# A one-core decoder block: layer norm by running sums less a pivot, and the shift sums of two GLU row blocks moved from TensorE to VectorE

## Chip, cores and metric

One Trainium2 chip, one core. The metric is device time in microseconds (us) of one execution; lower is better. Engines are TensorE (PE), VectorE (DVE), ScalarE (ACT), GpSimd (POOL) and SyncE (SP, which here only issues loads). All inputs are float32 in HBM, the input and output activations are 256 x 2048.

## What is computed

One layer of a hybrid decoder block and a final RMSNorm. Cut to what matters here:

```python
ada = (silu(c) @ w_ada + b_ada)            # (1, 6*2048)
sh1, sc1, g1, sh2, sc2, g2 = split(ada, 6)
h = rmsnorm(x, norm1_g) * (1 + sc1) + sh1
proj = h @ w_in                            # queries, keys, values, gates, GLU input, merge gates
y_a = attention(...) @ w_o_nsa
a, g = split(glu_in, 2)
u = a * sigmoid(g)                         # 256 x 2048
u = causal_dwconv(u, width 31) + bias
u = silu(layernorm over the 2048 channels (u) * ln_g + ln_b)
y_b = u @ conv_pw_w + b_pw
x = x + g1 * ((sigmoid(ga) * y_a + sigmoid(gb) * y_b) @ w_out)
h = rmsnorm(x, norm2_g) * (1 + sc2) + sh2
x = x + g2 * conv_ffn(h);  return rmsnorm(x, final_g)
```

## The kernel before

**Weights.** Every weight matrix is streamed once, in tiles of 128 x 1024 values (512 KB) that SP loads into `raw` (four buffers). ACT makes `hi`, the value rounded to the matmul's format (L227), DVE makes `lo`, the remainder (L228), three buffers each, and TensorE multiplies three times: activation-hi by hi, activation-hi by lo, activation-lo by hi (L249 to L251, L261 to L264; L282 and L283 pair two of them). There are 546 such tiles. Counted in the order of use: 64 for the GLU (1 to 64), 122 for keys, values, queries, the first merge gate and the attention's output product (65 to 186), 32 for the second merge gate `gbs` (187 to 218), 32 for `conv_pw_w` (219 to 250), 32 for `w_out` (251 to 282), then the FFN. Because there are three hi and three lo buffers, the tiles 219 to 221 can be split before TensorE is through with tile 218, and tile 221 only when tile 218 has been used.

**The GLU in four quarters.** The GLU's 64 tiles are taken in four row blocks (quarters) of 512 rows of `w_in`, because the rows of `h` become known a quarter at a time: `ada_quarter(q)` sums the shift and scale of quarter q from `w_ada` while the product of quarter q-1 runs. The scale side (side 1) is summed on DVE (`ada_dve`, L439, one fused multiply-add of 128 x 512 per 128 rows), the shift side (side 0) on TensorE (`ada_pe`, L421, matmuls with 32 weight columns, in four column groups). `modulate` then turns both into columns and makes the next rows of `h` (L375 to L378, L350, L351). `glu_out` adds each partial product in PSUM to `u` or `gl` (L390).

**Work in between.** The depthwise convolution, the layer norm and the other sums over `w_ada` are fillers: lists of small steps (`conv_q`, `ada_q`) with a declared cost. After each tile `tick` hands out steps as long as their engines' declared load is not ahead of TensorE's. An `ada_q` step loads one 128 x 1024 tile of `w_ada` into `araw` (two buffers, on the same SP queue as `raw`) and adds it on DVE (L298 first, then L301). Once `norm_only` is set, `ada_q` waits until `conv_q` is empty. A scheduler in the compiler then writes each engine's instruction order from its own time model; `high_priority` moves steps forward in it.

**Convolution.** `conv_blocks` takes three of the 16 channel blocks at a time (then the last alone): ACT multiplies by a tap (L559) and DVE adds (L568), or DVE does both (L549); the last tap writes the result back into `u` (L566). Two `cacc` buffers let two groups overlap.

**Layer norm.** After the last convolution group, DVE sums all 16 blocks (L880 to L886, then `half_sum`, L875 and L876), one matmul with ones gives the mean over channels, L898 subtracts it in place from all of `u`, ACT squares (L901), DVE sums, a second matmul (L909) gives the variance, eight 256-wide steps (L911 to L917) make the inverse deviation, L923 scales, ACT applies scale, bias and SiLU (L929), and L350 and L351 split the result into `uT`, the activation of the `conv_pw_w` product. `conv_done`, which is put before the layer norm, closes the convolution's pool, sets `norm_only`, and adds the 32 steps of the gate `g1` to the front of `ada_q`; their sums end in a matmul with ones (L326) and in `gb` (L327), which `residual` (L1010) needs in the `w_out` product. What is left of `conv_q` is emitted (`drain`) between tiles 218 and 219; what is left of the 32 gate steps, before `w_out`.

Of the kernel before, what the change touches and what calls it, by code (L numbers as in the profile page):

```python
# [59 lines left out]
def block_kernel(ctx, tc, x, c, w_ada, b_ada, norm1_g, w_in, cmp_pe, w_kc1, w_kc2, w_vc1, w_vc2,  # L60
# [82 lines left out]
    def give(q):  # L143
        cost, f = q.popleft()
        use(**cost)
        with ExitStack() as es:
            es.enter_context(tc.issue_after(los[0]))
            if q is heads_q:
                es.enter_context(tc.high_priority(HP))
            f()  # L150
# [250 lines left out]
    with tc.tile_pool(name="first", bufs=4) as first:  # L401
# [41 lines left out]
        def ada_quarter(q):  # L443
            box = {}
            js = range(q * KQ // 2, (q + 1) * KQ // 2)
            turns = [ada_dve(box, q, 1), (x for j in js for x in ada_pe(box, j, 0))]
            for _ in range(8):
                for g in turns:
                    next(g)
                    yield  # L450
            for g in turns:
                for _ in g:
                    pass
            for n, j in enumerate(js):
                modulate(j, halves(box[0, j]) + halves(box[1][:, n * T:(n + 1) * T]))
                yield
# [74 lines left out]
    MANY, FEW = tuple(s for s in range(2, CW) if s % 6) + (1,), tuple(range(6, CW, 4)) + (1,)  # L531

    def conv_blocks(b0, n, WIDE):

# [3 lines left out]
        def first(b):  # L538
            def f():
                if b == b0:  # L540
                    box["a"] = cvp.tile([P, n, T], F32, tag="cacc", name=nm("cacc"), bufs=2)
                nc.scalar.activation(box["a"][:, b - b0, :], u[:, b, :], AF.Identity, bias=cvb[:, b:b + 1],
                                     scale=cw[:, CW - 1, b:b + 1])
# [314 lines left out]
    def conv_done():  # L858

        cv.__exit__(None, None, None)  # L860
        norm_only[0] = True
        late = ctx.enter_context(tc.tile_pool(name="late", bufs=1))
# [4 lines left out]

    conv_q.append(({}, conv_done))


    lb = {}

    def half_sum(dst, a):

        nc.vector.tensor_add(a[:, 0:2, :], a[:, 0:2, :], a[:, 2:4, :])  # L875
        nc.vector.tensor_add(dst, a[:, 0, :], a[:, 1, :])  # L876

    def ln_mean1():
        lb["a"] = t4([P, 4, T])
        nc.vector.tensor_add(lb["a"], u[:, 0:4, :], u[:, 4:8, :])  # L880

    def ln_mean2():
        nc.vector.tensor_add(lb["a"], lb["a"], u[:, 8:12, :])

    def ln_mean3():
        nc.vector.tensor_add(lb["a"], lb["a"], u[:, 12:16, :])  # L886

    def ln_mean4():
        half_sum(lb["a"][:, 0, :], lb["a"])
        mp = pt([P, T])  # L890
        nc.tensor.matmul(mp, ones, lb["a"][:, 0, :], start=True, stop=True)
        lb["m"] = mp
        lb["q"] = t4([P, 4, T])

    def ln_centre(j):
        def f():
            v = u[:, 4 * j:4 * j + 4, :]
            nc.vector.scalar_tensor_tensor(v, lb["m"][:, None, :].to_broadcast([P, 4, T]), -1.0 / D, v,  # L898
                                           op0=ALU.mult, op1=ALU.add)
            s4 = t4([P, 4, T])  # L900
            nc.scalar.activation(s4, v, AF.Square)  # L901
            half_sum(lb["q"][:, j, :], s4)
        return f

    def ln_var():
        q = lb["q"]
        half_sum(q[:, 0, :], q)
        vp = pt([P, T])
        nc.tensor.matmul(vp, ones, q[:, 0, :], start=True, stop=True)  # L909
        ve = t4([P, 4, T])  # L910
        nc.vector.tensor_scalar(ve[:, 0, :], vp, 1.0 / D, EPS, op0=ALU.mult, op1=ALU.add)  # L911
        nc.scalar.activation(ve[:, 1, :], ve[:, 0, :], AF.Sqrt)
        nc.vector.reciprocal(ve[:, 2, :], ve[:, 1, :])
        nc.vector.tensor_mul(ve[:, 3, :], ve[:, 2, :], ve[:, 2, :])
        nc.vector.tensor_mul(ve[:, 3, :], ve[:, 3, :], ve[:, 0, :])
        nc.vector.tensor_scalar(ve[:, 3, :], ve[:, 3, :], -0.5, 1.5, op0=ALU.mult, op1=ALU.add)
        nc.vector.tensor_mul(ve[:, 3, :], ve[:, 3, :], ve[:, 2, :])  # L917
        lb["r"] = ve[:, 3, :]

    def ln_scale(j):  # L920
        def f():
            v = u[:, 4 * j:4 * j + 4, :]
            nc.vector.tensor_tensor(v, v, lb["r"][:, None, :].to_broadcast([P, 4, T]), op=ALU.mult)  # L923
        return f
# [7 lines left out]
    def ln_split(j):  # L932
        def f():
            if j == 0:
# [3 lines left out]
        return f  # L938

    conv_q.extend(({"dve": d, "act": a}, f) for d, a, f in  # L940
                  [(1130, 0, ln_mean1), (1130, 0, ln_mean2), (1130, 0, ln_mean3), (900, 0, ln_mean4)]
                  + [(2000, 1050, ln_centre(j)) for j in range(4)] + [(3000, 1700, ln_var)]
                  + [(1130, 0, ln_scale(0))]
                  + [i for j in range(4) for i in [(1130, 0, ln_scale(j + 1))] * (j < 3)
                     + [(0, LN_SILU, ln_silu(4 * j)), (0, LN_SILU, ln_silu(4 * j + 2))]])

# [194 lines left out]
```

## Time and profile before

| | |
|---|---|
| median of 3 runs | 1765.69 us (1760.31 to 1766.15) |
| the profiled execution | 1763.86 us, its span 1762.1 us |
| TensorE busy | 1696.0 us, 96% |
| VectorE busy | 1315.4 us, 75% |
| ScalarE busy | 992.1 us, 56% |
| loads | 403.85 MB read, 230 GB/s over the span |
| largest wait of TensorE | 16.3 us, one time, at 784.6 us |

The page gives busy time by engine and the chain of work that ended last. The waits name what an engine sat idle for. The timeline lists instructions in order of time with the idle time before each in square brackets. A table of stretches gives busy time, granted TensorE clock and DMA rate of each stretch.

### The profile page before, as it was taken

How to read it: one execution, taken by the hardware profiler on the slowest of the kernel's cores; microseconds unless marked ns; L12 is line 12 of the kernel's file. 1: busy time of each engine (PE TensorE's matmuls, PEld its weight loads, DVE VectorE, ACT ScalarE, POOL GpSimd, SP SyncE). 2: the span in 40 equal slices, each digit the busy share in tenths (PEclk: the TensorE clock that was granted, in tenths of full speed). 3: DMA queues.
4: the chain of work that ended last, by engine and by line, in shares of the span. 5: the costliest groups of instructions: out<-in, count | busy, mean ns of one | idle time of the engine just before them, and what ended most of it. 6: DMA issues, size and time to landing. Idle time of an engine off the chain costs nothing.

```text
span 1762.1 us, 26526 instructions
## 1 busy us (share of the span) xinstructions
PE 1696.0 (96%) x10148; PEld 1468.2 (83%) x10148; DVE 1315.4 (75%) x1722; ACT 992.1 (56%) x1506; POOL 6.2 (0%) x28
## 2 busy tenths in 40 slices
PE   6999999999999999987999899999999999999997
PEld 4899999999887778865877888888988888898886
DVE  2677698898878899988897677776577776576665
ACT  4443576885677778755344565554455554345553
POOL 0000000000000000000000000000000000000000
PEclk8999999999999999998999999999999999999998
DMA  9999788877557346778898577776677765566653
GB/s 342 321 352 321 233 276 273 269 249 215 178 163 245 131 150 209 238 227 279 312 315 298 180 229 225 221 223 221 223 225 222 220 215 180 191 191 189 189 191 124
DMA packets 264362, 407.68 MB, mean 231 GB/s; under 512 B 12684, under 2 KB 156844, under 8 KB 263596
## 3 DMA queue, kind: packets, MB, share of 16 engines
q1 hardware_dynamic: 261676, 399.44, 69.9%
q10 hardware_dynamic: 2560, 6.55, 1.1%
q8 instruction: 79, 1.29, 0.3%
q14 instruction: 47, 0.39, 0.1%
HBM read 403.85 MB, written 2.10 MB: 230 GB/s over the span
## 4 chain that ended last, share of the span: by engine, by line
PE 87%; DMA 5%; DVE 4%; ACT 2%; issue 2%; SPq 0%; ACTq 0%; DVEq 0%
PE accp L282 18%; PE accx L250 12%; PE accx L249 11%; PE accx L251 11%; PE accp L283 9%; PE accw L261 6%; PE accw L264 6%; PE accw L263 6%; DMA araw<-in_w_ada_dram 3%; DVE t L301 1%; PE pt L788 1%; DVE lo L228 1%; PE pt L421 1%; PE pt L827 1%; DMA araw<-in_w_kc_dram 1%
## 5 line engine op out<-in xcount | busy, mean ns | idle before, releaser
L227 ACT CAST hi<-raw 128x1024 fp32r<-128x1024 f32 x546 | 572.1, 1048 | 639.7 <-PE accx L251 266.7
L228 DVE TENSOR_TENSOR lo<-raw,hi 128x1024 fp32r<-128x1024 f32 x546 | 665.5, 1220 | 317.8 <-ACT hi L227 314.3
L282 PE MATMUL accp<-act,hi 128*128 128x512 f32 x1408 | 495.5, 397 | 0.2
L249 PE MATMUL accx<-hi,act 128*128 128x512 f32 (+2 forms) x1176 | 429.1, 366 | 18.3 <-ACT act L350 17.7
L250 PE MATMUL accx<-lo,act 128*128 128x512 f32 (+2 forms) x1176 | 435.0, 370 | 3.9 <-DVE lo L228 3.7
L251 PE MATMUL accx<-hi,act 128*128 128x512 f32 (+2 forms) x1176 | 429.3, 365 | 0.8 <-DVE act L351 0.8
L283 PE MATMUL accp<-act,lo 128*128 128x256 f32 x1408 | 395.2, 281 | 0.2 <-DVE lo L228 0.2
L282 PEld LDWEIGHTS accp<-act,hi 128*128 128x128 f32 x1408 | 264.2, 188 | 64.1 <-DVE act L351 0.8
L249 PEld LDWEIGHTS accx<-hi,act 128*128 128x128 f32 x1176 | 222.8, 189 | 55.1 <-ACT act L350 18.6
L283 PEld LDWEIGHTS accp<-act,lo 128*128 128x128 f32 x1408 | 266.0, 189 | 0.8 <-DVE lo L228 0.6
L261 PE MATMUL accw<-act,hi 128*128 128x256 f32 x896 | 259.1, 290 | 4.9 <-ACT accw L587 2.8
L250 PEld LDWEIGHTS accx<-lo,act 128*128 128x128 f32 x1176 | 222.9, 190 | 45.3 <-DVE lo L228 9.7
L263 PE MATMUL accw<-act,hi 128*128 128x256 f32 x896 | 258.0, 288 | 0.0
L264 PE MATMUL accw<-act,lo 128*128 128x256 f32 x896 | 257.6, 288 | 0.2 <-DVE lo L228 0.2
L251 PEld LDWEIGHTS accx<-hi,act 128*128 128x128 f32 x1176 | 223.0, 190 | 36.7 <-issue 1.7
L261 PEld LDWEIGHTS accw<-act,hi 128*128 128x128 f32 x896 | 174.8, 195 | 11.7 <-issue 3.9
L264 PEld LDWEIGHTS accw<-act,lo 128*128 128x128 f32 x896 | 174.5, 195 | 3.9 <-issue 3.1
L263 PEld LDWEIGHTS accw<-act,hi 128*128 128x128 f32 x896 | 174.6, 195 | 3.5 <-issue 3.0
L301 DVE SCALAR_TENSOR_TENSOR t<-araw,cs,t 128x1024 f32<-128x1024 f32 x120 | 153.5, 1279 | 19.2 <-DMA araw<-in_w_ada_dram 18.9
L559 ACT ACTIVATE cprod<-big,cw 128x230 f32<-128x230 f32 (+27 forms) x298 | 124.6, 487 | 13.4 <-DVE cacc L568 11.3
L568 DVE TENSOR_TENSOR cacc<-cacc,cprod 128x726 f32<-128x726 f32 (+28 forms) x110 | 87.6, 797 | 11.4 <-ACT cprod L559 8.2
L549 DVE SCALAR_TENSOR_TENSOR cacc<-big,cw,cacc 128x232 f32<-128x232 f32 (+24 forms) x182 | 77.6, 463 | 0.6
(208 smaller groups left out, 1051.2 us busy)
## 6 DMA issues: line engine op xcount, KB each, us to landing
araw<-in_w_ada_dram SPq DMA_DIRECT2D x192, 512.0 KB, 5.0
raw<-in_w_in_dram SPq DMA_DIRECT2D x180, 512.0 KB, 4.9
raw<-in_ffn_w_up_dram SPq DMA_DIRECT2D x176, 512.0 KB, 4.5
raw<-in_ffn_w_down_dram SPq DMA_DIRECT2D x88, 512.0 KB, 3.7
raw<-in_w_o_nsa_dram SPq DMA_DIRECT2D x32, 512.0 KB, 3.7
raw<-in_conv_pw_w_dram SPq DMA_DIRECT2D x32, 512.0 KB, 5.6
raw<-in_w_out_dram SPq DMA_DIRECT2D x32, 512.0 KB, 5.2
araw<-in_w_kc_dram SPq DMA_DIRECT2D x8, 512.0 KB, 5.6
```

The costliest lines, as they stand in the source:

```text
L227: nc.scalar.copy(hi[:, :n], raw[:, :n])
L228: los.append(nc.vector.tensor_tensor(lo[:, :n], raw[:, :n], hi[:, :n], op=ALU.subtract).ins)
L249: nc.tensor.matmul(o, act[:, k, 0, s], hi, start=k == 0, stop=False)
L250: nc.tensor.matmul(o, act[:, k, 0, s], lo, start=False, stop=False)
L251: nc.tensor.matmul(o, act[:, k, 1, s], hi, start=False, stop=k == nk - 1)
L261: nc.tensor.matmul(acc[:, b, :], hi[:, s], act[:, k, 0, :], start=begin and k == first and b % 2 == 0, stop=False, skip_group_check=True)
L263: nc.tensor.matmul(acc[:, b, :], hi[:, s], act[:, k, 1, :], start=False, stop=False, skip_group_check=True)
L264: nc.tensor.matmul(acc[:, b, :], lo[:, s], act[:, k, 0, :], start=False, stop=last, skip_group_check=True)
L282: nc.tensor.matmul(acc[:, b], hi[:, s], act[:, k], start=k == 0, stop=False, skip_group_check=True)
L283: nc.tensor.matmul(acc[:, b, 0, :], lo[:, s], act[:, k, 0, :], start=False, stop=k == KB - 1, skip_group_check=True)
L301: nc.vector.scalar_tensor_tensor(acc, raw, cs[:, k:k + 1], acc, op0=ALU.mult, op1=ALU.add)
L559: nc.scalar.mul(box["p"][:, b - b0, s:], u[:, b, :T - s], cw[:, CW - 1 - s, b:b + 1])
```

## The change

Three things are changed, all in the code above. (1) The shift sums of quarters 2 and 3 are made by `ada_dve` as well, so TensorE sums only quarter 1's. (2) The layer norm is computed by running sums: after the first convolution group a pivot (the mean of its three blocks) is found; each group, once convolved, has the pivot subtracted and is added, with its square, to two running sums `sq` while the convolution goes on; at the end one matmul gives both sums, the variance is mean of squares less squared mean, and `ln_scale` subtracts the mean and scales. (3) `cacc` has one buffer, `conv_done` and `norm_only` come after `ln_var`, and convolution-queue steps get high priority from then on.

```diff
-            if q is heads_q:
+            if q is heads_q or q is conv_q and norm_only[0]:
                 es.enter_context(tc.high_priority(HP))
...
+            on_pe = q < 2
+            turns = [ada_dve(box, q, 1), (x for j in js for x in ada_pe(box, j, 0)) if on_pe else ada_dve(box, q, 0)]
...
+                shift = box[0, j] if on_pe else box[0][:, n * T:(n + 1) * T]
+                modulate(j, halves(shift) + halves(box[1][:, n * T:(n + 1) * T]))
...
+    sq = cvp.tile([P, 2, T], F32, name="sq")
+    pivot = cvp.tile([P, T], F32, name="pivot")
+    def norm_sums(b0, n):
+        def sums(dst, a, fresh):
+            if fresh:
+                nc.vector.tensor_add(dst, a[:, 0, :], a[:, 1, :])
+            for j in range(2 if fresh else 0, n):
+                nc.vector.tensor_add(dst, dst, a[:, j, :])
+        def find():
+            sums(sq[:, 0, :], u[:, :n, :], True)
+            p_ = pt([P, T])
+            nc.tensor.matmul(p_, ones, sq[:, 0, :], start=True, stop=True)
+            nc.scalar.mul(pivot, p_, 1.0 / (n * P))
+        def less():
+            v = u[:, b0:b0 + n, :]
+            nc.vector.tensor_tensor(v, v, pivot[:, None, :].to_broadcast([P, n, T]), op=ALU.subtract)
+        def add():
+            v = u[:, b0:b0 + n, :]
+            s4 = t4([P, n, T])
+            nc.scalar.activation(s4, v, AF.Square)
+            sums(sq[:, 0, :], v, b0 == 0)
+            sums(sq[:, 1, :], s4, b0 == 0)
+        if b0 == 0:
+            conv_q.append(({"dve": 900, "act": 450, "pe": 250}, find))
+        conv_q.append(({"dve": 170 + n * 265}, less))
+        conv_q.append(({"dve": 840 * n, "act": 250 + 200 * n}, add))
...
-                    box["a"] = cvp.tile([P, n, T], F32, tag="cacc", name=nm("cacc"), bufs=2)
+                    box["a"] = cvp.tile([P, n, T], F32, tag="cacc", name=nm("cacc"))
...
+        norm_sums(b0, n)
...
     def conv_done():
-        norm_only[0] = True
...
     def ln_var():
+        norm_only[0] = True
+        vp = pt([P, 2, T])
+        nc.tensor.matmul(vp.rearrange("p a t -> p (a t)"), ones, sq.rearrange("p a t -> p (a t)"), start=True, stop=True)
         ve = t4([P, 4, T])
+        nc.vector.tensor_scalar(ve[:, 3, :], vp[:, 0, :], 1.0 / D, None, op0=ALU.mult)
+        nc.vector.tensor_mul(ve[:, 2, :], ve[:, 3, :], ve[:, 3, :])
+        nc.vector.scalar_tensor_tensor(ve[:, 0, :], vp[:, 1, :], 1.0 / D, ve[:, 2, :], op0=ALU.mult, op1=ALU.subtract)
+        nc.vector.tensor_scalar(ve[:, 0, :], ve[:, 0, :], EPS, None, op0=ALU.add)
...
     def ln_scale(j):
             v = u[:, 4 * j:4 * j + 4, :]
+            nc.vector.tensor_tensor(v, v, lb["m"][:, None, :].to_broadcast([P, 4, T]), op=ALU.subtract)
             nc.vector.tensor_tensor(v, v, lb["r"][:, None, :].to_broadcast([P, 4, T]), op=ALU.mult)
...
+    conv_q.append(({"dve": 5500, "act": 500}, ln_var))
+    conv_q.append(({}, conv_done))
```

The layer norm's old steps (`ln_mean1` to `ln_mean4`, `ln_centre`, `half_sum`) are gone.

The scheduler rewrites the order of every engine. Three places:

VectorE in the second GLU quarter (`asum` is a running sum over `w_ada`, `araw` its loaded tile, `accw` a GLU partial product). Before, from the fourth L390 of that quarter back:

```order
L439 SCALAR_TENSOR_TENSOR asum_1058<-araw_1302,cs,asum_1058 128x512
L228 TENSOR_TENSOR lo_1236<-raw_1234,hi_1235 128x1024
L439 SCALAR_TENSOR_TENSOR asum_1058<-araw_1302,cs,asum_1058 128x512
L439 SCALAR_TENSOR_TENSOR asum_1058<-araw_1374,cs,asum_1058 128x512
L228 TENSOR_TENSOR lo_1266<-raw_1264,hi_1265 128x1024
L439 SCALAR_TENSOR_TENSOR asum_1058<-araw_1374,cs,asum_1058 128x512
L390 TENSOR_TENSOR big_269<-big_269,accw_1155 128x1024
```

Now:

```order
L439 SCALAR_TENSOR_TENSOR asum_1058<-araw_1359,cs,asum_1058 128x512
L228 TENSOR_TENSOR lo_1226<-raw_1224,hi_1225 128x1024
L439 SCALAR_TENSOR_TENSOR asum_1063<-araw_1293,cs,asum_1063 128x512
L439 SCALAR_TENSOR_TENSOR asum_1058<-araw_1359,cs,asum_1058 128x512
L228 TENSOR_TENSOR lo_1256<-raw_1254,hi_1255 128x1024
L439 SCALAR_TENSOR_TENSOR asum_1063<-araw_1293,cs,asum_1063 128x512
L390 TENSOR_TENSOR big_269<-big_269,accw_1149 128x1024
L439 SCALAR_TENSOR_TENSOR asum_1058<-araw_1367,cs,asum_1058 128x512
L439 SCALAR_TENSOR_TENSOR asum_1063<-araw_1363,cs,asum_1063 128x512
```

Two running sums alternate where one stood; over the quarter twice as many L439 stand between the L228 of its 16 tiles.

VectorE at the end of the merge-gate product (the only L228 in each piece is tile 221's; `big_268` is `u`, `pt` the sums in PSUM, `t_1259` and `t_1275` the deviation's steps). Before, where the last convolution result (L566) had stood at tile 208:

```order
L911 TENSOR_SCALAR t_1259_7920<-pt_7918 128x256
L298 TENSOR_SCALAR t_1296_8159<-araw_8157,cs 128x1024
L913 RECIPROCAL t_1259_7920<-t_1259_7920 128x256
L301 SCALAR_TENSOR_TENSOR t_1296_8159<-araw_8161,cs,t_1296_8159 128x1024
L228 TENSOR_TENSOR lo_8237<-raw_8235,hi_8236 128x1024
L914 TENSOR_TENSOR t_1259_7920<-t_1259_7920 128x256
L301 SCALAR_TENSOR_TENSOR t_1296_8159<-araw_8182,cs,t_1296_8159 128x1024
L915 TENSOR_TENSOR t_1259_7920<-t_1259_7920 128x256
L301 SCALAR_TENSOR_TENSOR t_1296_8159<-araw_8208,cs,t_1296_8159 128x1024
L916 TENSOR_SCALAR t_1259_7920<-t_1259_7920 128x256
L917 TENSOR_TENSOR t_1259_7920<-t_1259_7920 128x256
L923 TENSOR_TENSOR big_268<-big_268,t_1259_7920 128x1024 x4
```

Now:

```order
L228 TENSOR_TENSOR lo_8216<-raw_8214,hi_8215 128x1024
L605 TENSOR_TENSOR cacc_7697<-cacc_7697,cprod_7955 128x229
L605 TENSOR_TENSOR cacc_7697<-cacc_7697,cprod_7958 128x228
L605 TENSOR_TENSOR cacc_7697<-cacc_7697,cprod_7961 128x227
L603 TENSOR_TENSOR big_268<-cacc_7697,cprod_7964 128x256
L556 TENSOR_TENSOR big_268<-big_268,pivot 128x256
L546 TENSOR_TENSOR sq<-sq,big_268 128x256
L546 TENSOR_TENSOR sq<-sq,t_1273_8010 128x256
L914 TENSOR_SCALAR t_1275_8016<-pt_8014 128x256
L929 TENSOR_TENSOR big_268<-big_268,t_1275_8016 128x1024 x2
L915 TENSOR_TENSOR t_1275_8016<-t_1275_8016 128x256
```

Behind the last row stand, now, two more L929, L916, L917, the reciprocal L919, L920 to L923, four L930 and four L351, and then tile 222. So the last convolution result (L603), the sums, the variance and the scaling all stand behind tile 221's L228, where L911 and L913 stood ahead of it; no gate step (L298, L301) stands among them, and the first of those now stands at tile 230 where it stood at tile 220.

SP's queue of loads in the `w_out` product (`raw` is a weight tile, `araw` a step over `w_ada`). Before, around its eighteenth `raw`:

```order
L224 DMA raw_9257<-in_w_out_dram 128x2x512
L295 DMA araw_9116<-in_w_ada_dram 128x1024
L224 DMA raw_9275<-in_w_out_dram 128x2x512
L295 DMA araw_9137<-in_w_ada_dram 128x1024
L224 DMA raw_9293<-in_w_out_dram 128x2x512
```

Now:

```order
L224 DMA raw_9264<-in_w_out_dram 128x2x512
L295 DMA araw_8935<-in_w_ada_dram 128x1024
L295 DMA araw_9011<-in_w_ada_dram 128x1024
L295 DMA araw_9039<-in_w_ada_dram 128x1024
L224 DMA raw_9282<-in_w_out_dram 128x2x512
L295 DMA araw_9060<-in_w_ada_dram 128x1024
L295 DMA araw_9081<-in_w_ada_dram 128x1024
L295 DMA araw_9084<-in_w_ada_dram 128x1024
L224 DMA raw_9309<-in_w_out_dram 128x2x512
```

From the eighteenth gate step to the last step over `w_ada` ahead of the second norm, 24 `araw` loads now stand with 19 `raw` loads, where 17 stood with the same 19; and the second L326, which waits for the 32nd gate step, stands on TensorE in tile 262, ahead of tiles 257 and 258, where it stood in tile 253.

## Rows read from the trace of the kernel before

**Rows 1.** The page, part 1: the span, then busy us (share) xinstructions of each engine

```profile
span 1762.1 us, 26526 instructions
...
PE 1696.0 (96%) x10148; PEld 1468.2 (83%) x10148; DVE 1315.4 (75%) x1722; ACT 992.1 (56%) x1506; POOL 6.2 (0%) x28
```

**Rows 2.** The page, part 4: shares of the chain that ended last, by engine

```profile
PE 87%; DMA 5%; DVE 4%; ACT 2%; issue 2%; SPq 0%; ACTq 0%; DVEq 0%
```

**Rows 3.** Waits on PE: waiter <- waited for: us in total, times, longest

```profile
PE accx L249 <- ACT act L350: 17.7, 2, 16.3
```

**Rows 4.** Stretches: PE, PEld, DVE, ACT, POOL busy; granted clock, DMA share, GB/s

```profile
92.85:201.99 109.14, 108.90 (x935) 100.50 (x934) 77.82 (x94) 43.40 (x53) 0.91 (x1) 1.00 0.91 302
202.00:784.60 582.60, 575.54 (x3532) 503.76 (x3530) 502.91 (x738) 421.51 (x785) 2.67 (x12) 0.99 0.69 219
784.60:800.90 16.30, 0.03 (x1) 0.04 (x1) 14.34 (x16) 10.87 (x16) 0.00 (x0) 0.66 0.64 211
800.90:838.00 37.10, 34.41 (x136) 26.60 (x137) 29.25 (x29) 17.54 (x22) 0.00 (x0) 0.92 0.87 304
838.00:950.00 112.00, 109.60 (x481) 86.74 (x480) 98.81 (x101) 45.03 (x51) 0.00 (x0) 1.00 0.91 315
```

**Rows 5.** The chain in order of time, third quarter start: start us, us, what

```profile
134.09 0.57 PE pt L421 x8
```

**Rows 6.** Groups by line: busy us, mean ns | idle before, releasers

```profile
L439 DVE SCALAR_TENSOR_TENSOR asum<-araw,cs,asum 128x512 f32<-128x512 f32 x45 | 33.7, 749 | 10.3 <-DMA araw<-in_w_ada_dram 9.7
L421 PE MATMUL pt<-araw,cz 128*32 128x256 f32 x320 | 29.1, 437 | 7.2 <-DMA araw<-in_w_ada_dram 6.4 <-ACT t L425 0.4 <-ACT big L490 0.4
```

**Rows 7.** Timeline of DVE, 751 to 803 us: start us, us, what, [idle before]

```profile
751.46 0.42 DVE L566 TENSOR_TENSOR big<-cacc,cprod 128x256 f32<-128x256 f32 x1
...
785.92 1.75 DVE L913 RECIPROCAL t<-t 128x256 f32<-128x256 f32 x1 [1.14 <-ACT t L912]
...
794.58 4.63 DVE L923 TENSOR_TENSOR big<-big,t 128x1024 f32<-128x1024 f32 x4
...
801.64 1.22 DVE L351 TENSOR_TENSOR act<-big,act 128x1024 fp32r<-128x1024 f32 x1
```

**Rows 8.** Timeline of ACT, 746 to 801 us

```profile
746.33 0.89 ACT L559 ACTIVATE cprod<-big,cw 128x227 f32<-128x227 f32 x2
...
784.18 1.28 ACT L912 ACT_TABLE_LOAD   x1 [1.68 <-PE pt L909]
785.47 0.42 ACT L912 ACTIVATE t<-t 128x256 f32<-128x256 f32 x1
785.79 1.03 ACT L227 CAST hi<-raw 128x1024 fp32r<-128x1024 f32 x1
...
788.13 1.02 ACT L959 ACTIVATE big<-accx 128x1024 f32<-128x1024 f32 x1
...
795.84 4.04 ACT L929 ACTIVATE big<-big,par 128x256 f32<-128x256 f32 x8 [5.39 <-DVE big L923]
799.78 1.03 ACT L350 CAST act<-big 128x1024 fp32r<-128x1024 f32 x1
```

**Rows 9.** Timeline of PE, 781 to 801 us

```profile
781.93 0.39 PE L249 MATMUL accx<-hi,act 128*128 128x512 f32 x1
...
782.61 0.39 PE L249 MATMUL accx<-hi,act 128*128 128x512 f32 x1
...
800.87 0.80 PE L249 MATMUL accx<-hi,act 128*128 128x512 f32 x1 [16.29 <-ACT act L350]
```

**Rows 10.** The chain in order of time, 840 to 950 us

```profile
849.62 0.87 PE pt L326 x2
```

**Rows 11.** Timeline of SP, 800 to 812 us

```profile
800.43 10.86 SPq L295 DMA_DIRECT2D araw<-in_w_ada_dram  x5
```

**Rows 12.** One stretch more, columns as in rows 4

```profile
825.00:850.00 25.00, 23.78 (x107) 19.13 (x107) 22.70 (x24) 11.03 (x12) 0.00 (x0) 1.00 0.98 358
```

**Rows 13.** The page, part 6: KB each, median us from issue to landing

```profile
araw<-in_w_ada_dram SPq DMA_DIRECT2D x192, 512.0 KB, 5.0
```

More of the change, by code (lines that the diff above doesn't have):

```diff
@@ L445, in ada_quarter @@
             js = range(q * KQ // 2, (q + 1) * KQ // 2)
-            turns = [ada_dve(box, q, 1), (x for j in js for x in ada_pe(box, j, 0))]
+            on_pe = q < 2
+            turns = [ada_dve(box, q, 1), (x for j in js for x in ada_pe(box, j, 0)) if on_pe else ada_dve(box, q, 0)]
             for _ in range(8):
@@ L454, in ada_quarter @@
             for n, j in enumerate(js):
-                modulate(j, halves(box[0, j]) + halves(box[1][:, n * T:(n + 1) * T]))
+                shift = box[0, j] if on_pe else box[0][:, n * T:(n + 1) * T]
+                modulate(j, halves(shift) + halves(box[1][:, n * T:(n + 1) * T]))
                 yield
@@ L866, in conv_done @@
             ada_q.extendleft(reversed(ada_steps(2 * D + i * WT, to_bcast(gate1["b"], 2 * D, i), 1500)))
-    conv_q.append(({}, conv_done))
     lb = {}
[L873 to L903, printed above, removed]
@@ L905, in ln_var @@
     def ln_var():
[L906 to L909, printed above, removed]
+        norm_only[0] = True
+        vp = pt([P, 2, T])
+        nc.tensor.matmul(vp.rearrange("p a t -> p (a t)"), ones, sq.rearrange("p a t -> p (a t)"), start=True, stop=True)
         ve = t4([P, 4, T])
-        nc.vector.tensor_scalar(ve[:, 0, :], vp, 1.0 / D, EPS, op0=ALU.mult, op1=ALU.add)
-        nc.scalar.activation(ve[:, 1, :], ve[:, 0, :], AF.Sqrt)
@@ L913, in ln_var @@
[L913 to L918, printed above, removed]
+        nc.vector.tensor_scalar(ve[:, 3, :], vp[:, 0, :], 1.0 / D, None, op0=ALU.mult)
+        nc.vector.tensor_mul(ve[:, 2, :], ve[:, 3, :], ve[:, 3, :])
@@ new lines, in ln_var @@
+        nc.vector.scalar_tensor_tensor(ve[:, 0, :], vp[:, 1, :], 1.0 / D, ve[:, 2, :], op0=ALU.mult, op1=ALU.subtract)
+        nc.vector.tensor_scalar(ve[:, 0, :], ve[:, 0, :], EPS, None, op0=ALU.add)
+        nc.scalar.activation(ve[:, 2, :], ve[:, 0, :], AF.Sqrt)
+        nc.vector.reciprocal(ve[:, 1, :], ve[:, 2, :])
+        nc.vector.tensor_mul(ve[:, 2, :], ve[:, 1, :], ve[:, 1, :])
+        nc.vector.tensor_mul(ve[:, 2, :], ve[:, 2, :], ve[:, 0, :])
+        nc.vector.tensor_scalar(ve[:, 2, :], ve[:, 2, :], -0.5, 1.5, op0=ALU.mult, op1=ALU.add)
@@ L920, in ln_scale @@
+        nc.vector.tensor_mul(ve[:, 2, :], ve[:, 2, :], ve[:, 1, :])
+        lb["m"], lb["r"] = ve[:, 3, :], ve[:, 2, :]
     def ln_scale(j):
@@ L938, in ln_split @@
         return f
+    conv_q.append(({"dve": 5500, "act": 500}, ln_var))
+    conv_q.append(({}, conv_done))
     conv_q.extend(({"dve": d, "act": a}, f) for d, a, f in
[L941 to L945, printed above, removed]
+                  [i for j in range(4) for i in [(2260, 0, ln_scale(j))]
+                   + [(0, LN_SILU, ln_silu(4 * j)), (0, LN_SILU, ln_silu(4 * j + 2))]])
     merged = bigt([P, NT, D])
```

## The prediction

> **What bounds the kernel now.** I read the span and the busy times first: TensorE is busy 1696.0 of 1762.1 us [rows 1], and the chain of work that ended last runs through TensorE for 87% of the span [rows 2]. So a saving counts only if it shortens TensorE's work or its waits, and a cost counts only if TensorE comes to wait for it. The waits of TensorE name one that matters, 16.3 us for the layer norm's split result [rows 3]; the timeline puts it between 784.6 and 800.87 us, ahead of the first product with `uT` [rows 9]. The table of stretches [rows 4] shows the rest: in the GLU quarters 2 and 3 (tiles 16 to 48) TensorE is busy 108.9 of 109.1 us and VectorE 77.8; from there to the wait VectorE is busy 502.9 of 582.6 us; behind the wait, in the two products that share SP's queue with the steps over `w_ada`, loads run at 304 to 315 GB/s, near the 358 GB/s of the fastest stretch I found [rows 12]. Three places, three terms.
>
> **Term 1, the GLU: -4 us.** The change takes 64 matmuls (2 quarters x 2 column blocks x 16) off TensorE. Each leaves two records (the code issues 160 in all, the rows show 320 [rows 6]), and eight records in a row take 0.57 us of the chain [rows 5]: 128 / 8 x 0.57 = 9.1 us. VectorE gains 2 x 16 = 32 multiply-adds of 128 x 512 at 0.749 us [rows 6], 24.0 us. If TensorE alone decided, the stretch would shrink from 109.1 to 100.0 us. But VectorE then has 77.8 + 24.0 = 101.8 us to do in it, and each `lo` of the 32 tiles and each L390, on which TensorE waits, stands behind more L439, which in turn wait for loads (before, they waited 9.7 us for them in all [rows 6]). Loads are no closer: 302 GB/s over 109.1 us are 33.0 MB, 92 us at 358 GB/s. So TensorE at 100.0 and VectorE at 101.8 stand level, and an in-order engine that is 97% full does not deliver on time. I take 105 us, a saving of 4. Ends: a saving of 9.1, if VectorE is never late; a loss of 4, if VectorE's waits of before (31.3 us idle in the stretch) take in only 20 of the new 24.0 us.
>
> **Term 2, the running sums: 0 us, but they shift the tail.** New on VectorE in the convolution are the subtraction of the pivot (16 blocks) and 32 additions of 256 columns (2 for the pivot, 30 for the two sums); at 0.42 us, the time of one 256-wide operation [rows 7], an upper estimate is 48 x 0.42 = 20.2 us. VectorE is idle 79.7 us between 202 and 784.6 us [rows 4], so TensorE pays nothing; were that cover gone, it would pay up to 20.2. What gets late instead is the convolution itself: its last result stands at tile 221 in the new order, where it stood at tile 208 and ended at 751.9 us [rows 7].
>
> **Term 3, the tail of the layer norm: +6 us.** The hi and lo buffers of tile 221 come free only when TensorE has used tile 218, at 784.6 us. In the new order the last convolution result and all of the layer norm's end stand behind that tile's `lo` on VectorE, so the whole chain runs while TensorE waits. Summed from there: ACT makes the tile's hi (1.03), the last sigmoid (1.02) and four products (0.89 for two, so 1.78) [rows 8]: 3.8. The last addition, the pivot, the square (priced as a product, 0.445) and the sum of squares are 0.42 + 0.42 + 0.445 + 0.42 [rows 7, 8]: 5.5. The matmul with ones over 512 columns: 0.87 for the two records of one such matmul, as the gate's have it [rows 10]: 6.4. Then on VectorE four 256-wide steps (1.68) and, in between, the four mean subtractions, priced as the four scalings (4.63) [rows 7]: 12.7. Square root on ACT 0.42 [rows 8], reciprocal 1.75 and four 256-wide steps 1.68 [rows 7]: 16.6. The first of four scalings 1.16, eight SiLU 4.04, the cast 1.03 [rows 7, 8]: 22.8 us, against 16.3 now. That is +6.5; consecutive records overlap a little, so +6. Ends: +7.8, if the 1.28 us of the table load ahead of the square root [rows 8] is not hidden behind VectorE; +4, if the overlaps are larger. What the change removes here (the sums and the centring, now between 752 and 784 us) lay beside TensorE's last gate tiles and cost nothing.
>
> **Term 4, the gate's steps: +10 us.** The 32 steps for `g1` are queued when `conv_done` runs and need one load of 0.524 MB and one L301 each. Before, nine of them and their first ran in the wait and the four tiles behind it. Now the first stands at tile 230, and those that are left are emitted in one go ahead of `w_out`: on SP's queue 24 `araw` loads stand with 19 `raw` loads where 17 stood before. 43 loads are 22.5 MB: 62.9 us at 358 GB/s, 71.5 at the 315 GB/s of the stretch from 838 to 950 us [rows 4, 12]. TensorE needs for 19 tiles of 12 matmuls, three in 0.68 us [rows 9], 19 x 2.72 = 51.7, and 1.7 for the two L326 pairs: 53.4 us. The difference is 9.5 to 18.1 us; up to four `raw` buffers, 4 x 2.72 = 10.9 us of lead, can be eaten first. L326 moreover stands on TensorE ahead of tiles 257 and 258 and waits for the 32nd step, and every `lo` behind an L301 waits with it. I take +10. Ends: 0, if the lead covers it all; +20, if it is gone by then and tiles 259 to 262 go through the one hi and lo buffer that 257 and 258 leave.
>
> For the same loads the row shows 5.0 us from issue to landing [rows 13]. The Trainium skill ("DMA: Bandwidth & Descriptors", the section on the anatomy of one DMA, fitted there to loads that GpSimd issues) has about 2.0 us and the bytes at 436 GB/s, an estimate of 3.2 us for 0.524 MB; with two buffers and 1.28 us of VectorE a step would then cost 2.2 us, 24 steps 54 us, and the burst would stay hidden. By it the sum would be 10 us lower. The row is longer than the rule, so I keep the rows' term.
>
> **Sum.** -4 + 0 + 6 + 10 = +12 us on the profiled execution's own 1763.86 us: **1776 us**. That execution lies 1.8 us below the median of the runs, so against the median it is +0.6%. A measurement of this kernel tells about 0.5% from no change, here 8.8 us.
>
> **Rivals.**
> (a) *The burst is hidden* (not slower). Place: tiles 250 to 270. Five gate loads issued back to back took 10.86 us from the first issue to the end of the fifth [rows 11], four intervals of about 2.6; 24 such steps are 63 us, against TensorE's 53.4, and the 10 us between are just what four `raw` buffers hold. It decides whether those buffers are full when the burst begins. Against it: the 24 loads alternate with 19 others on one queue. Without term 4 the time is 1766 us, no change.
> (b) *VectorE is less in TensorE's way* (faster). Place: all up to 784.6 us. The GLU gives its whole 9.1 us, and the new order also clears the 7.1 us that TensorE idles between 202 and 784.6 us [rows 4], and the burst is hidden by the same room: 1763.9 - 9.1 - 7.1 + 6 = 1754 us. For it: four ACT copies per quarter go too. Against it: VectorE has more to do in both stretches, not less.
> (c) *VectorE bounds the GLU, and the tail and the burst are at their upper ends*: +4 + 7.8 + 20, 1796 us. Point: VectorE above 95% busy in the GLU with TensorE waiting for `lo`.
> (d) That a part does nothing: the shift sums really leave TensorE and the two passes over `u` really go, the orders show it; nothing to weigh.
>
> **How the numbers follow.** The forecast (1770 to 1788) gets 0.48, (a) 0.27, (b) 0.15, (c) 0.10. Slower by over 0.5% is above 1774.5 us: 0.42 of the forecast and all of (c), 0.52. Within 0.5%: the rest of the forecast, 0.06, and 0.25 of (a), 0.31. Faster: (b) and 0.02 of (a), 0.17. The range of 1757 to 1791 us leaves out (b) and half of (c), 0.2. The forecast's own range is 1770 to 1788.
>
> **What would show it.** In the profile after: L421 down to 192 records, L439 up by 30, and the 32 tiles of the GLU's middle in 100 to 109 us with VectorE above 90% busy (term 1); the wait of TensorE ahead of the `conv_pw_w` product 20 to 24 us long, with the last convolution result after its beginning (term 3); the first L301 of the gate some 10 tiles into that product, and new waits of TensorE for `lo` or for L326 around tiles 255 to 268, 5 to 20 us together (term 4). The forecast is wrong if that first wait is shorter than 16 us, if those tiles pass without gaps, or if the GLU's stretch loses more than 7 us.

## The result, and the profile after

The changed kernel takes **1775.41 us** (median of 5 runs, 1774.69 to 1780.17), the kernel before in the same job 1765.69 us. The ratio is 1.0074, 95% interval 1.0048 to 1.0100: slower by 0.7%. The forecast was 1776 us, slower. The profiled execution took 1780.17 us, the longest of the five, with a span of 1778.5 us. It is read here for where time went, not for the last 5 us.

The page, part 1, answers to [rows 1], and the groups by line to [rows 6]:

```profile
span 1778.5 us, 26327 instructions
...
PE 1693.7 (95%) x10020; PEld 1468.6 (83%) x10020; DVE 1341.1 (75%) x1780; ACT 989.0 (56%) x1504; POOL 6.2 (0%) x28
```

```profile
L439 DVE SCALAR_TENSOR_TENSOR asum<-araw,cs,asum 128x512 f32<-128x512 f32 x75 | 54.7, 746 | 9.6 <-DMA araw<-in_w_ada_dram 9.4
L421 PE MATMUL pt<-araw,cz 128*32 128x256 f32 x192 | 17.8, 471 | 8.2 <-DMA araw<-in_w_ada_dram 6.1 <-ACT big L493 1.5 <-ACT t L425 0.5
```

L421 has lost 128 records, L439 has gained 30. VectorE works 25.7 us more in all, of which 18.8 lie in the GLU's quarters 2 and 3 (96.6 us below, 77.8 before [rows 4]). The new layer norm is not lighter for VectorE than the old one: alone, in the run ln_alone below, it raises VectorE's busy time by 7.8 us (to 1323.2).

The waits of TensorE, as in [rows 3]:

```profile
PE accx L249 <- ACT act L350: 16.8, 2, 16.4
PE accx L250 <- DVE lo L228: 8.4, 7, 2.9
...
PE pt L912 <- DVE sq L546: 5.8, 1, 5.8
PE accx L249 <- ACT hi L227: 4.8, 5, 1.1
```

The wait for the layer norm has become two, 5.8 us ahead of its matmul and 16.4 us behind it, and waits for `lo` and `hi` have come up. The stretches (PE, PEld, DVE, ACT, POOL busy; granted clock, DMA share, GB/s): GLU quarters 2 and 3, then up to tile 218, the layer norm's tail, and 40 us of the `w_out` product (the 253rd to the 260th tile in TensorE's order):

```profile
92.85:192.85 100.00, 98.20 (x812) 97.06 (x810) 96.57 (x122) 40.58 (x44) 0.00 (x0) 1.00 0.96 334
...
200.00:775.80 575.80, 568.23 (x3471) 497.91 (x3469) 496.04 (x743) 414.37 (x778) 2.52 (x10) 0.99 0.69 219
775.80:800.10 24.30, 2.09 (x3) 0.50 (x2) 18.89 (x27) 11.89 (x20) 0.10 (x1) 0.59 0.28 97
...
905.00:945.00 40.00, 28.99 (x94) 19.82 (x92) 27.82 (x25) 7.71 (x9) 0.00 (x0) 0.83 0.82 278
```

For the last of them, the same 40 us of the kernel before, in which TensorE gets from the 252nd to the 265th tile:

```profile
905.00:945.00 40.00, 38.55 (x166) 29.68 (x164) 35.24 (x36) 16.45 (x21) 0.00 (x0) 1.00 0.89 301
```

Tile 218 is done at 775.8 us, 8.8 us earlier than before. The tail gives 8.0 of that back (24.3 us against 16.3), so `conv_pw_w` begins at 800.1 us, where it began at 800.9. Then the two products ahead of the second norm take 15 us more (the last matmul of `w_out` ends at 1011.5 us, before at 997.0). Nine waits of TensorE for `lo`, `hi` or L326 lie between 906 and 941 us; in the 40 us it has 94 matmul records where it had 166, and the granted clock is 0.83 where it was 1.00.

How the tail runs: the timelines of VectorE, of ACT and of TensorE (columns as in [rows 7]):

```profile
776.92 1.22 DVE L228 TENSOR_TENSOR lo<-raw,hi 128x1024 fp32r<-128x1024 f32 x1 [0.16 <-ACT hi L227]
778.22 1.40 DVE L605 TENSOR_TENSOR cacc<-cacc,cprod 128x229 f32<-128x229 f32 x3
779.75 0.43 DVE L603 TENSOR_TENSOR big<-cacc,cprod 128x256 f32<-128x256 f32 x1
...
781.18 0.42 DVE L546 TENSOR_TENSOR sq<-sq,t 128x256 f32<-128x256 f32 x1
783.77 0.42 DVE L914 TENSOR_SCALAR t<-pt 128x256 f32<-128x256 f32 x1 [2.17 <-PE pt L912]
...
789.12 0.42 DVE L916 SCALAR_TENSOR_TENSOR t<-pt,t 128x256 f32<-128x256 f32 x1
...
790.34 1.75 DVE L919 RECIPROCAL t<-t 128x256 f32<-128x256 f32 x1 [0.48 <-ACT t L918]
...
793.84 4.63 DVE L930 TENSOR_TENSOR big<-big,t 128x1024 f32<-128x1024 f32 x4
```

```profile
785.11 1.28 ACT L918 ACT_TABLE_LOAD   x1 [3.97 <-issue]
789.89 0.42 ACT L918 ACTIVATE t<-t 128x256 f32<-128x256 f32 x1 [3.50 <-DVE t L917]
...
795.10 4.04 ACT L936 ACTIVATE big<-big,par 128x256 f32<-128x256 f32 x8 [3.48 <-DVE big L930]
799.04 1.03 ACT L350 CAST act<-big 128x1024 fp32r<-128x1024 f32 x1
```

```profile
781.66 2.08 PE L912 MATMUL pt<-sq,ones 128*128 128x512 f32 x2 [5.85 <-DVE sq L546]
800.12 0.80 PE L249 MATMUL accx<-hi,act 128*128 128x512 f32 x1 [16.39 <-ACT act L350]
```

The last convolution result (L603) ends 4.4 us after TensorE ran out of tiles, and everything behind it stands in one line. The table load lies beside VectorE's subtractions and costs nothing.

How the gate's steps run: pieces of the chain that ended last around 930 us (start, us, what), and SP's queue there:

```profile
927.08 0.79 PE accx L250
...
928.29 0.43 PE accx L249
...
930.41 0.24 PE accx L251
...
934.91 4.41 DMA araw<-in_w_ada_dram
939.42 1.28 DVE t L301
940.70 1.14 DVE lo L228
941.84 1.21 DVE t L301
943.06 6.36 DMA araw<-in_w_ada_dram
```

```profile
928.76 1.65 SPq L295 DMA_DIRECT2D araw<-in_w_ada_dram  x2
933.71 0.38 SPq L224 DMA_DIRECT2D raw<-in_w_out_dram  x1
934.91 6.14 SPq L295 DMA_DIRECT2D araw<-in_w_ada_dram  x3
941.86 0.38 SPq L224 DMA_DIRECT2D raw<-in_w_out_dram  x1
```

Three `araw` loads stand together on the queue with two buffers. The third waits for an L301 and the next `raw` behind it; L301 waits for its load (VectorE idles up to 3.2 us there; the two loads of `araw` above take 4.4 and 6.4 us of the chain), and `lo` stands behind L301 on VectorE. From 880 to 945 us, 47% of the chain is waiting for `araw`.

There is a second loop, between the engines. ACT's and TensorE's timelines:

```profile
924.72 1.04 ACT L227 CAST hi<-raw 128x1024 fp32r<-128x1024 f32 x1 [7.60 <-PE accx L251]
931.38 1.04 ACT L227 CAST hi<-raw 128x1024 fp32r<-128x1024 f32 x1 [5.62 <-PE accx L251]
```

```profile
924.29 0.39 PE L251 MATMUL accx<-hi,act 128*128 128x512 f32 x1
925.82 0.50 PE L249 MATMUL accx<-hi,act 128*128 128x512 f32 x1 [1.14 <-ACT hi L227]
927.08 0.79 PE L250 MATMUL accx<-lo,act 128*128 128x512 f32 x1 [0.76 <-DVE lo L228]
```

From 916 to 940 us `hi` of the next tile is written only when TensorE has ended the tile before, as with a single buffer. The last matmuls of three tiles in a row start at 924.29, 930.95 and 937.68 us, 6.7 us apart; at the pace of [rows 9], three matmuls in 0.68 us, a tile of twelve takes 2.7. This fits the order: the second L326 stands ahead of tiles 257 and 258, whose `hi` and `lo` hold two of the three buffers until the 32nd gate step has come. Of the 11.0 us that TensorE waits in the 40 us, 6.1 belong to this loop (four waits for `hi`, two for `lo` behind it), 3.8 to `lo` behind an L301, and 1.1 to L326.

### The profile page after: what moved, and what is told of

Read it like the earlier page. It is cut to its first block, busy times and chain, and to the rows that moved or that the text cites. A ratio compares the mean times of both kernels' runs of the same rounds, so it can differ in the third digit from the quotient of the medians.

```text
span 1778.5 us, 26327 instructions
## 1 busy us (share of the span) xinstructions
PE 1693.7 (95%) x10020; PEld 1468.6 (83%) x10020; DVE 1341.1 (75%) x1780; ACT 989.0 (56%) x1504; POOL 6.2 (0%) x28
## 4 chain that ended last, share of the span: by engine, by line
PE 81%; DMA 7%; DVE 6%; ACT 3%; issue 2%; SPq 0%; DVEq 0%; ACTq 0%
PE accp L282 19%; PE accx L250 11%; PE accx L249 11%; PE accx L251 11%; PE accp L283 9%; DMA araw<-in_w_ada_dram 6%; PE accw L261 5%; PE accw L264 5%; PE accw L263 5%; DVE lo L228 2%; PE pt L826 1%; DVE t L301 1%; DVE asum L439 1%; DMA araw<-in_w_kc_dram 1%; PE pt L865 1%
## 5 line engine op out<-in xcount | busy, mean ns | idle before, releaser
L228 DVE TENSOR_TENSOR lo<-raw,hi 128x1024 fp32r<-128x1024 f32 x546 | 665.5, 1220 | 300.0 <-ACT hi L227 297.5
L249 PEld LDWEIGHTS accx<-hi,act 128*128 128x128 f32 x1176 | 223.9, 190 | 61.5 <-ACT act L350 18.8
L301 DVE SCALAR_TENSOR_TENSOR t<-araw,cs,t 128x1024 f32<-128x1024 f32 x120 | 153.6, 1280 | 28.1 <-DMA araw<-in_w_ada_dram 27.7
L586 DVE SCALAR_TENSOR_TENSOR cacc<-big,cw,cacc 128x232 f32<-128x232 f32 (+24 forms) x182 | 77.8, 464 | 0.6
```

The lines of the kernel that those rows point to most:

```text
L228: los.append(nc.vector.tensor_tensor(lo[:, :n], raw[:, :n], hi[:, :n], op=ALU.subtract).ins)
L249: nc.tensor.matmul(o, act[:, k, 0, s], hi, start=k == 0, stop=False)
L301: nc.vector.scalar_tensor_tensor(acc, raw, cs[:, k:k + 1], acc, op0=ALU.mult, op1=ALU.add)
```

## The experiments

The theory is the prediction's four terms, after the profile of the changed kernel: GLU about -7, running sums 0, tail +8, and the burst of late gate steps +10 to +13. Its main rivals: the loss is VectorE's added work, not the order; or the burst is hidden. Ratios are against the kernel before in the same job (its median 1764.8, 1762.8, 1763.4 and 1762.0 us in the four jobs that follow). Where runs of two jobs are compared by their ratios, a ratio is turned into us at 1764 us.

**glu_alone.** The kernel before, with the diff's part on `on_pe` and nothing else.

> The kernel before with the shift sums of quarters 2 and 3 on VectorE and the old layer norm. Theory (the four terms of the prediction, sized by the profile of the changed kernel: GLU about -7, tail +8, gate burst +10 to +13 us): the GLU's saving stands alone, 1757 to 1761 us (-5 to -9), L421 down to 192 records, the wait ahead of the conv_pw_w product 16 us as before. Rival (VectorE, now almost full in the GLU, gives the saving back later, as late convolution steps): 1764 to 1767 us.

1754.91 us, ratio 0.9942 (0.9924 to 0.9961): -9.8 us. The wait ahead of `conv_pw_w` is 16.3 us, unchanged. The stretch of 100 us:

```profile
92.85:192.85 100.00, 98.12 (x811) 97.04 (x811) 96.57 (x122) 40.88 (x44) 0.00 (x0) 1.00 0.96 333
```

VectorE is 97% busy and TensorE still 98%. The 9.8 us are, within the interval, the 9.1 that the GLU's matmuls cost, and the rival falls.

**ln_alone.** The changed kernel with `on_pe = True`.

> The changed kernel with the shift sums of all quarters left on TensorE: the running sums, the one cacc buffer and the late gate steps alone. Theory: the loss of tail and burst without the GLU's gain, 1781 to 1786 us (+15 to +20 on before), the wait ahead of the conv_pw_w product 23 to 25 us, waits for lo and for L326 at tiles 255 to 268 of 10 us together. Rival (the loss comes from VectorE being made late in the GLU): 1766 to 1772 us, with the wait near 16 us.

1786.67 us, ratio 1.0122 (1.0102 to 1.0141), within a microsecond of the theory's upper end. The wait from tile 218 to `conv_pw_w` is 24.3 us, and the waits for `lo`, `hi` and L326 from 905 us on are there. Tail and burst belong to the new layer norm's order, not to the GLU.

**gate_early.**

```diff
     drain(conv_q)
+    load["dve"] = load["pe"]
```

> The changed kernel, with VectorE's declared load set level with TensorE's where the convolution's queue is drained, so that the gate's first step stands at tile 221 instead of 230 and no burst stands at tile 260; the tail of the layer norm is untouched. Theory (the burst is term 4's cost): 10 to 13 us faster than the changed kernel, 1763 to 1766 us, no wait for L326 and the 24-to-19 burst gone. Rival (the burst is hidden by the raw buffers; what costs there is VectorE's total work): 1774 to 1777 us, the same waits at other tiles.

1762.70 us, ratio 0.9983 (0.9972 to 0.9995): 12.7 us below the changed kernel by the medians, 16 by the ratios. The same two stretches:

```profile
771.30:803.00 31.70, 2.12 (x3) 0.55 (x3) 25.30 (x34) 11.95 (x20) 0.10 (x1) 0.55 0.55 174
...
905.00:945.00 40.00, 38.93 (x168) 30.24 (x167) 35.68 (x36) 16.31 (x20) 0.00 (x0) 1.00 0.91 313
```

The gate's steps make the tail even longer, 31.7 us, but the burst is gone and TensorE is whole again behind 905 us. Only the places of the steps are changed; the number of VectorE's instructions (1780) is the same, its busy time 1338.9 us against 1341.1. Over glu_alone 7.8 us are left in the same job. They are not the tail alone: by the two traces the wait is 15.4 us longer than in glu_alone, but tile 218 is done 4.7 us earlier, and the two products behind the wait, with fewer gate steps to share the queue with, take 5.4 us less.

**gate_late.** The other way round: glu_alone, its old layer norm untouched, and the gate's steps held back.

```diff
     drain(conv_q)
+    load["dve"] = load["pe"] + 16000.0
```

> The kernel of glu_alone (old layer norm) with VectorE's declared load set 16 us ahead of TensorE's after the convolution's queue is drained: two gate steps stand at tile 220, the next at tile 230, and a burst of 24 such loads as in the changed kernel forms behind tile 258. No arithmetic is added. Theory (the late gate steps by themselves cost 10 to 13 us): 1764 to 1769 us, against 1754.9 for glu_alone, with waits for hi, lo and L326 at tiles 255 to 270. Rival (the burst costs only together with the running sums): 1754 to 1758 us.

1763.67 us, ratio 1.0013 (0.9998 to 1.0028): 8.8 us over glu_alone by the medians, 12.5 by the ratios. Two stretches of 40 us, of glu_alone first, then of gate_late (the waits for `lo` and `hi` lie there, the longest 4.1 us):

```profile
895.00:935.00 40.00, 37.47 (x162) 28.89 (x161) 35.36 (x38) 16.70 (x21) 0.00 (x0) 1.00 0.90 306
```

```profile
895.00:935.00 40.00, 30.98 (x117) 23.00 (x117) 30.84 (x30) 9.47 (x10) 0.00 (x0) 0.91 0.84 284
```

The two products behind the wait take 205.4 us, in glu_alone 196.3. The burst costs by itself, with no running sums in the program.

**conv_early.** The running sums are declared cheap, so the planner hands the convolution out faster.

```diff
-        conv_q.append(({"dve": 170 + n * 265}, less))
-        conv_q.append(({"dve": 840 * n, "act": 250 + 200 * n}, add))
+        conv_q.append(({"dve": 100}, less))
+        conv_q.append(({"dve": 100, "act": 250}, add))
```

> The changed kernel with the running sums declared at almost no cost, so that the planner deals out the convolution faster: its last result stands at tile 213 (after: 221), and the gate's steps begin at tile 216. Nothing is computed otherwise. Theory (late order, not work, makes the tail long and the burst): wait ahead of the conv_pw_w product 15 to 18 us, no burst, together 1753 to 1759 us. Rival (the added work on VectorE is the cost, so handing it out earlier makes lo late between tiles 100 and 213): TensorE waits for lo there of 8 us and more, 1766 us or above.

1765.05 us, ratio 1.0000 (0.9987 to 1.0014). Ten us better than the changed kernel by the medians, but neither expectation is met. The burst is gone and the wait is 18.5 us, hardly over the range. But TensorE reaches that wait at 783.3 us, 7.3 later than in glu_alone, and its waits for `lo` come to 6.8 us over the 800 us from 200 to 1000, too few for the rival. Between 500 and 650 us it has 1.2 us less busy time and a granted clock of 0.97 against 0.98. That is 1.2 us and about 1.5 us (an estimate, 0.01 of 150) of the 7.3; the rest was not found.

**old_early.** The old layer norm with the convolution handed out faster: glu_alone and

```diff
-            conv_q.append(({"dve": 170 + n * 265}, wide(s)))
+            conv_q.append(({"dve": 170 + n * 210}, wide(s)))
```

> The kernel of glu_alone (old layer norm) with the wide convolution additions declared at 800 instead of 965 ns for three blocks, about what the trace has (0.80 us): the last convolution result stands at tile 196 instead of 208, the layer norm's scaling at tile 215 instead of 221, its split results at tiles 217 to 219. Theory (an order that leaves VectorE's idle time in front of the tail costs the wait): the 16 us wait ahead of the conv_pw_w product falls below 5 us, 1738 to 1746 us. Rival (VectorE has no room between tiles 64 and 218, so what is dealt earlier makes lo late, as in conv_early): 1750 to 1757 us, TensorE idle over 20 us between 200 and 780 us.

1772.16 us, ratio 1.0057 (1.0044 to 1.0071). The wait did fall: two waits for `lo` of 3.7 us each are left there, at 781 and 795 us. But the time rose over glu_alone, by 17 us by the medians and 20 by the ratios. Neither expectation names why. The stretch, and SP's queue in it:

```profile
905.00:945.00 40.00, 27.76 (x90) 21.10 (x89) 20.82 (x21) 7.45 (x8) 0.00 (x0) 0.74 0.70 240
```

```profile
914.15 2.89 SPq L295 DMA_DIRECT2D araw<-in_w_ada_dram  x2
918.16 0.38 SPq L224 DMA_DIRECT2D raw<-in_w_out_dram  x1
920.18 6.00 SPq L295 DMA_DIRECT2D araw<-in_w_ada_dram  x3
926.99 0.38 SPq L224 DMA_DIRECT2D raw<-in_w_out_dram  x1
928.18 2.88 SPq L295 DMA_DIRECT2D araw<-in_w_ada_dram  x2
```

The same burst has formed with other steps over `w_ada`, and TensorE is 10.8 us less busy in these 40 us than before, at a clock of 0.74.

**sums_early.** conv_early with old_early's line.

> The kernel of conv_early (running sums, declared at almost no cost) with the wide convolution additions declared at 800 instead of 965 ns: last convolution result at tile 204, the variance at tile 210, scaling at tile 215, splits at tiles 217 to 219. Theory (the order is all that is wrong with the running sums): the wait ahead of the conv_pw_w product below 5 us, 1738 to 1748 us, level with old_early. Rival (their work on VectorE makes lo late between 300 and 780 us, as conv_early's loss of 7 us there suggests): 8 us or more above old_early.

1774.39 us, ratio 1.0066 (1.0052 to 1.0080). With nearly the same order as old_early, the running sums cost 0.1% more, within both intervals; the rival's 8 us did not come in the time. They did come, nearly, ahead of the tail: ACT splits tile 218 at 790.5 us, in old_early at 783.2, and 4.5 of these 7.3 us are made up by the end of the `w_out` product. The waits there are down to 3.8 us and less, and the burst is there too.

**glu_all.** glu_alone with `on_pe = q < 1`.

> The kernel of glu_alone with the shift sums of quarter 1 on VectorE as well. Theory (TensorE's matmul time is what the GLU pays, VectorE at 95% delivers on time): another 32 matmuls of two records, 4.5 us less, 1749 to 1752 us. Rival (quarter 1 stands beside the start of the loads, where TensorE waits for data and not for its own work): 1754 to 1757 us.

1752.33 us, ratio 0.9942 (0.9929 to 0.9956), the same ratio as glu_alone, whose before was 1.9 us slower. By the ratio the rival's time holds: to move quarter 1's matmuls gained nothing that can be measured here. Its reason is not what the trace shows. ACT splits tile 32 at 140.5 us, 3.2 earlier than in glu_alone, but tile 48 1.5 us later, and in the 100 us from 92.85 TensorE waits 4.4 us for `lo`, in glu_alone 1.6.

**pace6000, pace5000, pace4500.** glu_all with old_early's line, and `PACE`, the loads' declared cost of a step over `w_ada` ahead of the merge gate, changed from 6500:

> The kernel of glu_all (old layer norm, all shift sums but the first lead on VectorE) with the wide convolution additions declared at 800 ns, as in old_early, and the steps over w_ada paced at 6000 instead of 6500 ns of loads. Last convolution result at tile 202, scaling at tiles 218 and 219, 28 of the 96 steps over w_ada behind tile 230 (glu_all 30). Theory (both the order of the tail and the even spread of the steps count): the wait ahead of the conv_pw_w product falls from 16.5 to 8 to 11 us, six loads in four tiles behind tile 262 cost 2 to 5 us: 1744 to 1750 us. Rival (any faster dealing of the convolution is paid by waits elsewhere): 1753 us or more.

> As pace6000 with 5000 ns: last convolution result at tile 212, scaling at tile 220, 20 of the 96 steps over w_ada behind tile 230, none behind tile 262. Theory: the wait ahead of the conv_pw_w product as in glu_all (15 to 17 us), no wait for lo or hi of over 1 us from 850 us to the second norm: 1749 to 1752 us. Rival (ten more steps over w_ada between tiles 100 and 190 make lo late there): 1754 us or more.

> As pace6000 with 4500 ns: last convolution result at tile 209, scaling at tile 221, 16 of the 96 steps over w_ada behind tile 230, none behind tile 250. Theory: the wait ahead of the conv_pw_w product 16 to 18 us, the w_out product free of steps: 1748 to 1752 us. Rival (as for pace5000): 1754 us or more.

1768.49 us (ratio 1.0027, 1.0015 to 1.0039), 1757.89 (0.9979, 0.9969 to 0.9990) and 1769.43 (1.0034, 1.0019 to 1.0049): all three above the theory. In pace6000 the wait was 8.0 us as expected, but TensorE was idle 12.9 of the 150 us from 500 to 650, against 3.9 in glu_all, in the attention, and the burst was there again. In the other two the wait grew to 24 and 28 us, from tile 218's end, as the layer norm's last sum (L878) had become late. Earlier steps only moved the waits.

**spread.** glu_all with old_early's line, and the steps that are left behind the merge gate handed out at half the rate.

```diff
-    hurry = [(dict(cost, dma=1500), f) for cost, f in ada_q]
+    hurry = [(dict(cost, dma=3000), f) for cost, f in ada_q]
```

> The kernel of glu_all with the wide convolution additions declared at 800 ns, as in old_early, and the steps over w_ada that are left behind the merge gate paced at 3000 instead of 1500 ns of loads. Last convolution result at tile 195, scaling at tile 214, splits at tiles 217 to 219; behind tile 250 the loads of the steps never stand two in a row but once, where old_early has groups of three. Theory (two places decide: VectorE's order in front of the tail and the spread of the steps' loads): the wait ahead of the conv_pw_w product below 6 us and no wait for hi or lo over 2 us behind 850 us: 1738 to 1746 us. Rival (the early convolution pays in the attention instead, as in pace6000): TensorE idle over 15 us between 500 and 640 us, 1750 us or more.

**1743.67 us, ratio 0.9900 (0.9883 to 0.9916)**, faster than both kernels. TensorE has no wait for the layer norm's split result left, only short ones for `lo`:

```profile
778.76 0.54 PE L250 MATMUL accx<-lo,act 128*128 128x512 f32 x1 [2.57 <-DVE lo L228]
...
793.53 0.50 PE L250 MATMUL accx<-lo,act 128*128 128x512 f32 x1 [1.54 <-DVE lo L228]
```

and none from 905 to 945 us:

```profile
905.00:945.00 40.00, 40.00 (x178) 33.14 (x177) 30.39 (x31) 19.87 (x25) 0.00 (x0) 1.00 0.88 305
```

It is idle 8.0 us from 500 to 650, so the rival's place is seen, at half its size. The kernel uses the old layer norm. It was measured on glu_all with old_early's line; the halved rate alone, without that line, was not run.

## Why the prediction was right

**Sum.** Forecast +12 on the profiled 1763.86 us, measured +9.7 by the medians and +13 by the ratio. It came out on the number because one saving and two costs were each put too low, by about the same in sum. That nearness is luck; the place and the direction of each term were right.

**Term 1, the GLU, -4: mis-sized.** It measured -9.8 us (glu_alone), the upper end of 9.1. The step that failed is "an in-order engine that is 97% full does not deliver on time". VectorE was 96.6 of 100 us busy, TensorE 98.2; the waits for `lo` in the stretch add up to 1.2 us, and to 1.6 in glu_alone (longest 0.9). That three `lo` buffers evened it out is likely, but no run changed them. The premise of a VectorE at 101.8 us was off as well: the 32 new steps raised its busy time by 18.8 us, not 24.0, since two multiply-adds back to back take 1.41 us in the trace and not twice 0.75, and the first step of each sum takes 0.48 us. And of the 9.7 us that L439 had waited for loads, only 0.9 lay in this stretch.

**Term 2, the running sums, 0: right.** VectorE is busy 496.0 of the 575.8 us from 200 to 775.8, before 502.9 of 582.6 [rows 4], and tile 218 is done at 775.8 us, in glu_alone at 776.0. That the convolution's end gets late instead was seen: L603 ended at 780.2 us. Where the convolution is dealt out faster the term is not nothing: sums_early reaches the tail 7.3 us behind old_early, though 0.1% is all that is left of it in the time.

**Term 3, the tail, +6: right in mechanism, a little short.** 24.3 us against the 22.8 that were summed. The matmul with ones took 2.08 us for its two records where [rows 10] had 0.87: TensorE had waited 5.85 us, and the granted clock of the stretch is 0.59. That is 1.2 of the 1.5. The table load was hidden, as the middle value had it. Against the 16.3 us before, the tail costs 8.0 us, just over the upper end. This is read from the traces of after and ln_alone (24.3 us in both); no run changes the tail alone.

**Term 4, the gate's steps, +10: right, and short.** gate_early gives 12.7 us (16 by the ratios), gate_late 8.8 (12.5); in the trace the two products take 15.3 us more than before. The first L298 came at 830.1 us, ten tiles into the product, and from 869.9 to 940.9 us eleven waits of over 0.5 us for `lo`, `hi` and L326 add up to 13.7 us. The working compared loads with TensorE's need and found 9.5 to 18.1 us less a lead. But the loads ran at 278 GB/s in the 40 us, below the 315 and 358 of the working, so their rate is not what was full. What the trace shows is more local: VectorE waits at an L301 for its load, up to 3.2 us, and `lo` waits behind it; and four tiles in a row go through one pair of hi and lo buffers, which the working named only for its end of +20. And it left the clock out: the records behind the waits that ended at 920.6, 927.1 and 933.7 us stand 0.43 us apart, then 0.24.

Two buffers, and a load of 5.1 us from issue to landing (the median of after; [rows 13] had 5.0), likely set the pace of a group of steps. spread, with the same two buffers and its loads one by one, had no wait in these 40 us; the number of buffers was not varied. By the Trainium skill ("DMA: Bandwidth & Descriptors", the section on the anatomy of one DMA, a fit to loads that GpSimd issues) an estimate is 3.2 us for the same bytes, by which the burst would have stayed hidden and the sum been 10 us lower. The trace does not agree, on a queue that is shared with the weights.

**Rivals.** (a) fell with gate_early and gate_late: the burst is not hidden. (b) had the GLU right, all 9.1 us, and the rest wrong. (c) fell in its first part: VectorE was above 95% busy in the GLU, and TensorE waited 1.2 us for `lo`, not 4 us and more.

**Open:** the 4 to 5 us that remain in conv_early ahead of 783 us, and the 7.3 us of sums_early. No run took the high priority away by itself, the second `cacc` buffer was not tried with the running sums, and no run parts the grouped loads from the place of L326.

## What to carry to other kernels

Removing passes that lie beside the bounding engine's work saved nothing here; what it did to the order and to the planner's declared load was the change. Look where the postponed steps land: 32 loads in the wrong place cost more (15.3 us in the trace) than the layer norm's longer tail (8.0), and two changed declared costs brought spread 0.4% (0.9942 to 0.9900) on top of the GLU's 0.6%. Clearing one wait pays only if the work that it sets free has an even place to go, so read SP's queue for loads in groups larger than their buffers, and TensorE's order for a waiting step that stands ahead of tiles already split.

## What the runs showed of the hardware

In the burst TensorE's lower clock cost over half as much as the waits themselves. A stretch without long idle time had a granted clock of 1.00 (905 to 945 us before). With waits of 0.8 to 2.9 us in pairs, from 916 us on some 7 to 9 us apart, as in the burst, it was 0.83, and 0.74 in old_early. Behind the wait that ended at 927.1 us the records of the chain stood 0.43 us apart, and from 930.4 us on 0.24 us, as at the lower and at the higher of the clock's two levels (1.2 and 2.4 GHz). Over the stretch from 905 to 945 us 0.17 x 40 = 6.8 us of full speed are missing (an estimate, a little high, as TensorE was idle in part of the slow time), beside 11.0 us of idle time.

VectorE, 97% busy and in order, held TensorE up for only 1.2 us in 100 in the GLU, where its 122 instructions were all of 1.3 us or less (4.4 us in glu_all, at 96%). The same engine was in the way at 70% busy (27.8 of 40 us) where it stood waiting for a load. What counted most was for what it could be made to wait.
